# Banded attention in a fused transformer layer: the row maxima are transposed a unit later, behind the score products, and their products are moved a unit later

## The chip, the cores and the metric

The kernel runs on one core of one Trainium2 chip. The metric is the device time of one execution in microseconds. A profile of one execution shows each engine's instructions: PE (matmul), PEld (weight load), DVE, ACT, POOL and SP, which here only issues DMAs.

## What is computed

One layer of a transformer: modulation, RMSNorm, one input projection, two groups of attention heads, an output projection, a mixture of 16 experts, and a final norm. The change lies in head group A, banded attention with a sink in the softmax. For each block of 128 queries and each of 2 key groups (4 heads share the keys):

```python
keys = jnp.concatenate([kc, kb], axis=1)      # 256 context keys, 384 keys of the band
s = jnp.einsum('bqkgd,bskd->bkgqs', qb, keys) * (DH_A ** -0.5) + bias
p = jax.nn.softmax(jnp.concatenate([s, s_sink], axis=-1), axis=-1)[..., :-1]
o = jnp.einsum('bkgqs,bskd->bqkgd', p, vals)
```

Softmax needs a maximum of every query row before the exponential is taken.

## The kernel before

Banded attention is 16 blocks (8 of 128 queries for each key group; a block holds 4 heads, so 512 columns). A block is a run of 4 or 5 **units**, one for each 128 keys; there are 76 units. The numbers of a block's first unit are U0 = 0, 4, 9, 14, 19, 24, 29, 34, 38, 42, 47, 52, 57, 62, 67, 72.

`Runner.run` (L591) writes the instruction order by hand. In unit u it first emits what was registered for that unit (`at[u]`), then the unit's scores (`s_a`, L759), then the subtraction `lo` of the unit before, then the value products of unit u-3 (`pv_a`, L774). Every engine takes its instructions in the order in which they are emitted, and so does SP's queue of DMAs. An instruction that waits holds all that stands behind it on its engine.

The scores are two products, or three with the mask: L765 with the queries, L766 with a 65-row operand `ql` whose last row holds the negated maximum, and L768 with the mask. ACT then takes two exponentials (L614, L615). So **row 64 of `ql` has to be there before L766 of the block's first unit**.

`prep_blk(i)` (L665) makes that row, for block i while block i-2 is worked on, in nine steps. The list `OFFS` (L899) says at which unit after U0[i-2] each step stands; the three lists are for 10, 9 and 8 units from U0[i-2] to U0[i]:

- `tr`: 4 transposes on PE (L677), copy on ACT (L678). `low`: two DVE operations (L681, L682).
- `mxc(0)`, `mxb(0)`; `mxb(1)`; `mxc(1)`, `mxb(2)`; `mxb(3)`: six products on PE (L687, L695), each reduced to maxima on DVE (L689, L699).
- `fin`: two small DVE operations that give `nm` (L707, L708).
- `fin2`: PE transposes `nm` (L712), ACT copies it into `rr` (L714), SP issues two DMAs: `rr` into row 64 of `ql` (L715), and `rr` into `e` (L720).
- `fin3`: ACT takes the exponential of `e` (L724).

After the last value product of a block, `blk_finish` (L735) registers three steps. The product stands at unit U0+2 of the next block, and the steps 1, 3 and 6 units on: `s0` (a DMA from ACT's queue, L741), `s1` (DVE L744, L745; SP issues L746, then L748, which waits for L746 to land) and `s2` (POOL multiplies, L751; SP issues the block's output, L732, which waits for that). In terms of the block that is being prepared, `s2` of block i-3 stands at U0[i-2]+8.

All small PSUM tiles (`m`) share three banks in turn. The rest of the time goes to filling work in `at[u]`: in the first half the query up-projection `q_up` (L633) and `ka_prep` (L622), in the second `ckv_trans`, `kn_mm` and `v_mm`.

Of the kernel before, what the change touches and what calls it, by code (L numbers as in the profile page):

```python
# [38 lines left out]
def f32(ap):  # L39
    return ap.bitcast(F32)  # L40
# [7 lines left out]
def tile_backbone(ctx: ExitStack, tc, x, c, ctxt, c_ctx, w_mod, b_mod, norm_attn, norm_ffn, w_in,  # L48
# [107 lines left out]
    def bank(tag, shape=(128, 512)):  # L156
        return psa.tile(list(shape), F32, tag, bufs={"s": 3, "x": 2, "m": 3}[tag])
# [425 lines left out]
    class Runner:  # L583
# [4 lines left out]
        def add(self, u, f):  # L588
            self.at.setdefault(u, []).append(f)

        def run(self, units, emit_s, emit_pv, la):  # L591
            n = len(units)
            st = {}
            for u in range(n + la):
                self.u = u
                for f in self.at.pop(u, []):
                    f()
                if u < n:
                    st[u] = emit_s(u, units[u])
                if 1 <= u <= n:  # L600
                    st[u - 1][2]()
                if u >= la:
                    emit_pv(u - la, units[u - la], st.pop(u - la))
            late = [f for u in sorted(self.at) for f in self.at[u]]
            self.at = {}
            return late
# [48 lines left out]
    units = []  # L655
# [6 lines left out]
    HALF = U0[NT]  # L662
    R = Runner()

    def prep_blk(i):  # L665
        g, b = BL[i]
        st = {}

        def tr():
            st["q"] = q2 = pa.tile([128, 512], F32R, "q2", bufs=3)  # L670
            st["l"] = pa.tile([65, 512], F32R, "ql", bufs=3)
            st["x"] = pa.tile([128, 4, 2], F32, "mx", bufs=3)
            QA[i] = (q2, st["l"])
            pt = st["p"] = bank("m")
            for j in range(4):
                h = 4 * g + j
                pe.transpose(pt[0:64, j * 128:(j + 1) * 128], qa[:, b, h * 64:(h + 1) * 64], ident)  # L677
            act.activation(q2[0:64], pt[0:64], AF.Copy)  # L678

        def low():  # L680
            dve.tensor_copy(st["q"][64:128], f32(st["q"][0:64]))  # L681
            dve.tensor_sub(st["l"][0:64], st.pop("p")[0:64], f32(st["q"][0:64]))  # L682

        def mxc(a):
            pm = bank("m").rearrange("p (a b) -> p a b", a=2)
            for j in range(2):
                pe.matmul(pm[:, j], st["q"][:, (2 * a + j) * 128:(2 * a + j + 1) * 128], kst[g][:, 0:256],  # L687
                          start=True, stop=True)
            dve.tensor_reduce(out=st["x"][:, 2 * a:2 * a + 2, 0], in_=pm, axis=AX.X, op=OP.max)  # L689

        def mxb(j):
            j0, j1 = max(b - 1, 0), min(b + 2, NT)
            n = (j1 - j0) * 128
            pm = bank("m")
            pe.matmul(pm[:, :n], st["q"][:, j * 128:(j + 1) * 128],  # L695
                      kst[g][:, (NCT + j0) * 128:(NCT + j1) * 128], start=True, stop=True)
            junk = pa.tile([128, 384], F32, "mjunk")
            mo = j0 - (b - 1)
            dve.tensor_tensor_reduce(out=junk[:, :n], in0=pm[:, :n],  # L699
                                     in1=mq[:, mo:mo + (j1 - j0)].rearrange("p a b -> p (a b)"),  # L700
                                     scale=1.0, scalar=-3e38, op0=OP.add, op1=OP.max,
                                     accum_out=st["x"][:, j, 1:2])

        def fin():
            v = pa.tile([128, 4], F32, "mv", bufs=2)
            st["n"] = nm = pa.tile([128, 4], F32R, "nm", bufs=3)
            dve.tensor_max(v, st["x"][:, :, 0], st["x"][:, :, 1])  # L707
            dve.scalar_tensor_tensor(nm, v, -1.0, nsink8[:, 4 * g:4 * g + 4], op0=OP.mult, op1=OP.min)  # L708

        def fin2():  # L710
            pt = bank("m")
            pe.transpose(pt[:4, :128], f32(st["n"]), ident)  # L712
            rr = pa.tile([4, 128], F32R, "rr", bufs=2)
            act.activation(rr, pt[:4, :128], AF.Copy)  # L714
            nc.sync.dma_start(out=f32(st["l"][64:65, :]), in_=f32(rr))  # L715
            if i == len(BL) - 1:
                NM[i] = st["n"]
            else:
                E4[i] = pa.tile([128, 4], F32, "e4", bufs=3)
                nc.sync.dma_start(out=E4[i], in_=f32(rr))  # L720

        def fin3():
            if i < len(BL) - 1:
                act.activation(E4[i], E4[i], AF.Exp, scale=SC_A, bias=sinkp[:, g:g + 1])  # L724

        return [tr, low, lambda: (mxc(0), mxb(0)), lambda: mxb(1), lambda: (mxc(1), mxb(2)), lambda: mxb(3),
                fin, fin2, fin3]

    def blk_out(i, ou):
# [133 lines left out]
    def kr_pe(t0, t1):  # L863
        pt = bank("s")
        for t in range(t0, t1):
            pe.transpose(pt[:32, (t - t0) * 128:(t - t0 + 1) * 128], kr[:, t], ident)
        return pt
# [11 lines left out]
    def v_mm(t):  # L879
        pt = bank("m")  # L880
        for k in range(2):
# [5 lines left out]
    Q = [lambda t=t, g=g: q_up(t, g) for t in range(NT) for g in range(2)]  # L887
    CQ1 = [lambda k=k: cq_split(1, k, cq_pe(1, k, "m")) for k in range(3)]
    p0, p1 = prep_blk(0), prep_blk(1)
    NQP = 6  # L890
    pre = [Q[0], lambda: ka_prep(0, 0, 4), p0[0], Q[1], lambda: va_prep(0, 5), p0[1], p0[2], p0[3], Q[2], p0[4], p0[5],
           p1[0], Q[3], p0[6], lambda: ka_prep(0, 4, 8), p1[1], p0[7], Q[4],
           lambda: dve.tensor_copy(vah[:, :, :, 64], ones[:, 0:2 * NK].rearrange("p (a b) -> p a b", b=2)),
           p1[2], p1[3], last_scaled, p1[4], Q[5], p0[8]]
    for f in pre:
        f()
    for d, f in zip((0, 1, 1, 4), p1[5:]):
        R.add(d, f)
    OFFS = {10: (0, 1, 2, 3, 4, 5, 6, 7, 10), 9: (0, 1, 2, 3, 4, 5, 5, 6, 9), 8: (0, 1, 2, 2, 3, 4, 4, 5, 8)}  # L899
    for i in range(2, len(BL)):  # L900
        for d, f in zip(OFFS[U0[i] - U0[i - 2]], prep_blk(i)):
            R.add(U0[i - 2] + d, f)
# [12 lines left out]
        R.add(HALF + 3 + i * (len(units) - HALF - 5) // NKV, KV[i])  # L915
    KV = KV[NKV:]

    late = R.run(units, s_a, pv_a, 3)
    krt = [kr_pe(*g) for g in TG]
    for f in late:  # L920
        f()
# [96 lines left out]
    units = [(h, hf, kc, kc == 0, kc == NK - 1) for h in range(HB) for hf in range(2) for kc in range(NK)]  # L1018
# [803 lines left out]
```

## Time and profile before

| | |
|---|---|
| Time, median of 3 runs | 1213.65 us (1212.35 to 1213.77) |
| The profiled execution's own time | 1211.27 us |
| Its span, first to last instruction | 1209.6 us |
| PE busy | 1108.7 us (92% of the span) |
| DVE, ACT, POOL busy | 880.3, 702.6, 464.2 us |
| Banded attention, first to last score product | 232.5 to 401.5 us |

Busy time is a share of the whole span, over stages with different limits. For the change only the stage from 232 to 403 us matters, and the idle time of the engine that sets its pace.

### The profile page before, as it was taken

The numbers are of one execution on the slowest core, as the hardware profiler recorded it, in microseconds if no ns is written. First come the engines' busy times: TensorE is split into PE (matmuls) and PEld (weight loads), VectorE is DVE, ScalarE is ACT, GpSimd is POOL, SyncE is SP. The second block draws the span as 40 slices with busy tenths as digits, with TensorE's granted clock in tenths as the row PEclk, the third lists the DMA queues.
The fourth block names the chain that finished last, engine by engine and source line by source line (L and its number), as shares of the span: only waits on it lengthen the run. The fifth ranks groups of instructions, "written<-read, shape, count | busy, mean of one in ns | idle before, by whom it ended". The sixth has DMA issues, their size and how long they took to land. (4 is left out here: it accounts for less than half of the span.)

```text
span 1209.6 us, 15354 instructions
## 1 busy us (share of the span) xinstructions
PE 1108.7 (92%) x5168; PEld 833.1 (69%) x5168; DVE 880.3 (73%) x1509; ACT 702.6 (58%) x1124; POOL 464.2 (38%) x453
## 2 busy tenths in 40 slices
PE   7799998899899889999999999996499999999993
PEld 1587886677567667776766677885377887778871
DVE  5767764565884376776778255488789999999987
ACT  5633223467776567776776762323176776777754
POOL 0042221456443244665655432442214243332214
PEclk9899999899999999999999999997599999999997
DMA  8714320001211120212010535645799999999827
GB/s 303 286 67 132 116 90 1 1 15 23 62 28 23 27 85 22 88 53 88 19 44 16 182 91 200 236 187 218 277 324 368 376 363 390 373 394 370 290 44 286
DMA packets 68622, 198.27 MB, mean 164 GB/s; under 512 B 15894, under 2 KB 24243, under 8 KB 63423
## 3 DMA queue, kind: packets, MB, share of 16 engines
q1 hardware_dynamic: 60224, 178.73, 40.6%
q0 software_dynamic: 5152, 18.52, 5.8%
q8 instruction: 40, 0.66, 0.2%
q10 hardware_dynamic: 3168, 0.06, 0.1%
q14 instruction: 38, 0.31, 0.1%
HBM read 172.34 MB, written 24.78 MB: 163 GB/s over the span
## 5 line engine op out<-in xcount | busy, mean ns | idle before, releaser
L1417 DVE TENSOR_TENSOR wl<-wst,wh 128x2048 fp32r<-128x2048 f32 x95 | 216.1, 2289 | 22.2 <-ACT wh L1411 22.2
L1411 ACT ACTIVATE wh<-wst 128x2048 fp32r<-128x2048 f32 x96 | 183.9, 1917 | 71.7 <-PE u L1588 40.0
L614 ACT ACTIVATE ph<-s 128x512 fp32r<-128x512 f32 x236 | 140.7, 596 | 91.4 <-PE s L1103 74.1
L1106 POOL TENSOR_TENSOR pl<-pf,ph 128x512 fp32r<-128x512 f32 x76 | 102.3, 1356 | 64.9 <-ACT pf L615 53.2
L1106 DVE TENSOR_TENSOR pl<-s,ph 128x512 fp32r<-128x512 f32 x84 | 57.0, 680 | 54.1 <-ACT s L615 54.1
L986 DVE TENSOR_REDUCE mx<-m 128x1 f32<-128x512 f32 x128 | 83.1, 682 | 10.5 <-PE m L984 10.2
L615 ACT ACTIVATE s<-s 128x512 f32<-128x512 f32 x123 | 73.1, 594 | 0.0
L1634 PE MATMUL y<-wh,shf 128*128 128x512 f32 x240 | 69.4, 400 | 0.0
L1099 PE MATMUL s<-ql,kh 96*128 96x512 f32 x160 | 65.1, 407 | 2.7 <-DVE pl L1106 2.7
L772 POOL TENSOR_TENSOR pl<-pf,ph 128x512 fp32r<-128x512 f32 x37 | 47.5, 1285 | 50.6 <-ACT pf L615 47.3
L615 ACT ACTIVATE pf<-s 128x512 f32<-128x512 f32 x113 | 66.9, 592 | 0.0
L122 POOL TENSOR_SCALAR rstd<-ss 128x1 f32<-128x1 f32 x36 | 13.1, 363 | 134.9 <-ACT sjunk L193 65.2
L1103 PE MATMUL s<-qh,kh 97*128 97x512 f32 x160 | 63.3, 396 | 1.3 <-DMA qh<-rr 1.3
L1115 PE MATMUL x<-ph,vh 128*65 128x512 f32 x160 | 63.2, 395 | 0.0
L1100 PE MATMUL s<-qh,kl 96*128 96x512 f32 x160 | 63.1, 394 | 0.0
L1117 PE MATMUL x<-pl,vh 128*65 128x512 f32 x160 | 63.0, 393 | 0.0
L1116 PE MATMUL x<-ph,vh 128*64 128x512 f32 x160 | 62.9, 393 | 0.0
L329 PE MATMUL s<-wih,hb 128*128 128x512 f32 (+2 forms) x224 | 57.0, 376 | 3.2 <-ACT hb L81 3.2
L1556 POOL DMA_INDIRECT xg<-h2d,ix x16 | 23.6, 1472 | 91.5 <-PE t L1572 36.4
L1651 POOL DMA_INDIRECT accd<-yt,ix x7 | 34.7, 4958 | 61.2 <-DVE yt L1644 61.2
L81 ACT ACTIVATE hb<-xt 128x512 fp32r<-128x512 f32 (+1 forms) x22 | 13.0, 593 | 69.3 <-DVE xt L245 69.2
L984 PE MATMUL m<-kh,qh 96*128 96x512 f32 x128 | 47.0, 412 | 5.8 <-ACT kn L877 3.8
(491 smaller groups left out, 3105.7 us busy)
## 6 DMA issues: line engine op xcount, KB each, us to landing
wst<-in_w_gate_dram SPq DMA_DIRECT2D x63, 512.0 KB
wst<-in_w_up_dram SPq DMA_DIRECT2D x63, 512.0 KB
wst<-in_w_down_dram SPq DMA_DIRECT2D x31, 1024.0 KB
mw<-in_w_mod_dram SPq DMA_DIRECT2D x32, 256.0 KB
wst<-in_w_mod_dram SPq DMA_DIRECT2D x8, 1024.0 KB
wi<-in_w_in_dram SPq DMA_DIRECT2D x8, 720.0 KB
wi<-in_w_mod_dram SPq DMA_DIRECT2D x9, 512.0 KB
h2d<-h SPq DMA_DIRECT2D x8, 520.0 KB
```

What stands on the lines that cost most here:

```text
L614: act.activation(ph, ps, AF.Exp, scale=scale)
L615: act.activation(pf, ps, AF.Exp, scale=scale)
L986: dve.tensor_reduce(out=st["m"][:, t, j:j + 1], in_=pm, axis=AX.X, op=OP.max)
L1099: pe.matmul(ps, kh[0:96, ks], ql[:, qs], start=True, stop=False)
L1100: pe.matmul(ps, kl[:, ks], qh[0:96, qs], start=False, stop=False)
L1103: pe.matmul(ps, kh[:, ks], qh[:, qs], start=False, stop=True)
L1106: return ph, lo, lambda: (dve if on_dve else pool).tensor_sub(lo, pf, f32(ph))
L1115: pe.matmul(xx, vv[:, kc, 0:65], ph, start=first, stop=False)
L1117: pe.matmul(xx, vv[:, kc, 0:65], lo, start=False, stop=last)
L1411: act.activation(W[i][0], staged[i], AF.Copy)
L1417: eng.tensor_sub(lo, staged.pop(i), f32(hi))
L1634: pe.matmul(py[n], a[:, k], w[b][:, n], start=(k == 0 and m == 0), stop=(k == 3 and m == 2))
```

## The change

The step `fin2` no longer emits its instructions. It puts them (as `fin2b`) on a list, which `Runner.run` empties right behind the unit's scores. In the list of first steps ahead of the runner, the list is emptied after each step, so there the order is as before. The offsets in `OFFS` change: the products of the maxima stand up to a unit later, `fin` stands in the unit of the last of them, and `fin2` a unit later than before.

```diff
-        def run(self, units, emit_s, emit_pv, la):
+        def run(self, units, emit_s, emit_pv, la, between=None):
...
                 if u < n:
                     st[u] = emit_s(u, units[u])
+                if between:
+                    between()
                 if 1 <= u <= n:
                     st[u - 1][2]()
...
+    LATER = []
...
         def fin2():
+            LATER.append(fin2b)
+
+        def fin2b():
             pt = bank("m")
             pe.transpose(pt[:4, :128], f32(st["n"]), ident)
...
+    def after_s():
+        while LATER:
+            LATER.pop(0)()
+
     for f in pre:
         f()
+        after_s()
...
-    OFFS = {10: (0, 1, 2, 3, 4, 5, 6, 7, 10), 9: (0, 1, 2, 3, 4, 5, 5, 6, 9), 8: (0, 1, 2, 2, 3, 4, 4, 5, 8)}
+    OFFS = {10: (0, 1, 3, 4, 5, 6, 6, 8, 10), 9: (0, 1, 3, 4, 4, 5, 5, 7, 9), 8: (0, 1, 3, 3, 4, 4, 4, 6, 8)}
...
-    late = R.run(units, s_a, pv_a, 3)
+    late = R.run(units, s_a, pv_a, 3, after_s)
```

The third offset is that of the first products, the seventh that of `fin`, the eighth that of `fin2`, the ninth that of `fin3`.

## Rows read from the trace of the kernel before

**Rows 1.** Busy time by stage: the start and end of the stretch, its length, then for each engine the busy time and the number of instructions, the granted clock of PE, the DMA share and GB/s. The two halves of banded attention, and the dense attention after it.

```profile
232.00:318.00 86.00, 80.93 (x414) 58.71 (x413) 58.64 (x149) 63.01 (x131) 47.80 (x69) 1.00 0.10 18
318.00:403.00 85.00, 80.30 (x381) 55.79 (x380) 55.88 (x137) 62.10 (x126) 34.96 (x28) 0.98 0.17 39
435.00:730.00 295.00, 286.45 (x1282) 200.97 (x1281) 197.22 (x294) 208.51 (x384) 163.27 (x125) 1.00 0.23 75
```

**Rows 2.** What PE waited for from 215 to 402 us: us in total, times, longest.

```profile
PE m L712 <- DVE nm L708: 3.9, 5, 1.4
PE m L687 <- DVE q L681: 1.8, 5, 0.7
...
PE m L687 <- DVE ql L682: 1.0, 1, 1.0
PE m L637 <- ACT rr L714: 0.8, 2, 0.6
```

**Rows 3.** The same waits one by one, on PE's timeline (start, duration, engine, line, operation, tiles, shape, and in brackets the idle time before it and what ended it): a value product of block 0, and block 2.

```profile
237.94 0.44 PE L783 MATMUL x<-pl,vah 128*65 128x512 f32 x1 [0.70 <-POOL pl L772]
...
243.49 0.27 PE L712 MATMUL m<-ident,nm 128*4 128x128 f32 x1 [0.70 <-DVE nm L708]
```

**Rows 4.** PE's timeline, block 10's maxima.

```profile
331.30 0.27 PE L712 MATMUL m<-ident,nm 128*4 128x128 f32 x1 [1.44 <-DVE nm L708]
```

**Rows 5.** PE's timeline, block 12's time: a product of maxima that waits.

```profile
353.42 0.50 PE L687 MATMUL m<-ks,q 128*128 128x256 f32 x2 [0.66 <-DVE q L681]
```

**Rows 6.** All engines' timeline, block 11's maxima and the DMAs at the end of block 8.

```profile
341.18 0.32 SPq L746 DMA_DIRECT2D rcd<-l  x1
...
341.46 0.27 PE L712 MATMUL m<-ident,nm 128*4 128x128 f32 x1 [0.72 <-DVE nm L708]
...
342.64 0.49 SPq L748 DMA_DIRECT2D rbc<-rcd  x1
...
342.71 0.47 PE L687 MATMUL m<-ks,q 128*128 128x256 f32 x2 [0.98 <-DVE ql L682]
```

**Rows 7.** All engines' timeline: block 10's DMA behind another, unit 45's last exponential, and the product that needs the DMA.

```profile
334.73 0.46 SPq L748 DMA_DIRECT2D rbc<-rcd  x1
335.28 0.64 SPq L715 DMA_DIRECT2D ql<-rr  x1
...
335.61 0.59 ACT L615 ACTIVATE s<-s 128x512 f32<-128x512 f32 x1
...
337.81 0.40 PE L766 MATMUL s<-ql,k 65*128 65x512 f32 x1
```

**Rows 8.** PE's timeline, scores of unit 17 and of unit 19, the first of block 4.

```profile
273.05 0.40 PE L765 MATMUL s<-q,kn 128*128 128x512 f32 x1
...
278.43 0.40 PE L766 MATMUL s<-ql,vb 65*128 65x512 f32 x1
```

**Rows 9.** SP's timeline, the DMAs of block 4's maxima (L715, L720) and what follows them: L732 is the output of block 1.

```profile
268.44 0.64 SPq L715 DMA_DIRECT2D ql<-rr  x1
269.13 0.60 SPq L720 DMA_DIRECT2D e<-rr  x1
276.64 0.65 SPq L732 DMA_DIRECT2D mixd<-ou  x1
```

**Rows 10.** POOL's timeline, the product ahead of that output.

```profile
275.33 1.29 POOL L751 TENSOR_TENSOR ou<-ou,rbc 64x512 f32<-64x512 f32 x1
```

**Rows 11.** ACT's timeline: last exponential of unit 27, and `fin3` of block 6.

```profile
301.13 0.59 ACT L615 ACTIVATE s<-s 128x512 f32<-128x512 f32 x1
...
302.60 0.31 ACT L724 ACTIVATE e<-e,sinkp 128x4 f32<-128x4 f32 x1
```

**Rows 12.** PE's timeline: the first L766 of blocks 6 and 7.

```profile
301.72 0.40 PE L766 MATMUL s<-ql,vb 65*128 65x512 f32 x1
...
311.15 0.39 PE L766 MATMUL s<-ql,vb 65*128 65x512 f32 x1
```

**Rows 13.** SP's timeline: the DMAs at the end of block 4.

```profile
304.52 0.32 SPq L746 DMA_DIRECT2D rcd<-l  x1
306.48 0.49 SPq L748 DMA_DIRECT2D rbc<-rcd  x1
...
310.73 0.65 SPq L732 DMA_DIRECT2D mixd<-ou  x1
```

**Rows 14.** All engines' timeline, the output of block 8 and the first L766 of block 11.

```profile
347.67 0.65 SPq L732 DMA_DIRECT2D mixd<-ou  x1
...
350.15 0.39 PE L766 MATMUL s<-ql,k 65*128 65x512 f32 x1
```

**Rows 15.** All engines' timeline, block 14: last exponential of unit 65, and the first L766 of the block.

```profile
382.69 0.59 ACT L615 ACTIVATE s<-s 128x512 f32<-128x512 f32 x1
...
385.93 0.39 PE L766 MATMUL s<-ql,k 65*128 65x512 f32 x1
```

**Rows 16.** ACT's timeline there: `fin3` of block 4 and the copy that stands behind it.

```profile
276.55 0.30 ACT L724 ACTIVATE e<-e,sinkp 128x4 f32<-128x4 f32 x1
276.82 0.59 ACT L678 ACTIVATE q<-m 64x512 fp32r<-64x512 f32 x1
```

**Rows 17.** Busy time by stretch, columns as in Rows 1: before and in a stretch at half the clock.

```profile
338.00:343.70 5.70, 4.00 (x21) 2.43 (x20) 4.17 (x11) 3.96 (x9) 3.60 (x3) 1.00 0.12 23
343.70:347.10 3.40, 3.40 (x11) 2.09 (x10) 2.49 (x8) 2.15 (x4) 0.73 (x1) 0.50 0.15 47
```

## Prediction

> **What bounds the kernel now.** I read the stages first. Banded attention takes 171 us, and in both halves PE is the busiest engine, 80.93 of 86 and 80.30 of 85 us, while ACT, next, has 63.01 and 62.10. The dense attention behind it is bound by PE too, 286.45 of 295 us [rows 1]. So a microsecond that PE gains or loses in the banded stage should reach the end. I take it one to one; less is possible, more isn't shown.
>
> Then I read what PE waits for in this stage. 3.9 us go to the transposition of the maxima, which stands on PE ahead of DVE's result. 1.8 and 1.0 us go to the first products of the maxima, which wait for the lower halves of the queries, and 0.8 us to a PSUM bank that the copy `rr` held: 7.5 us in all [rows 2]. That is the most that the change can take away. Last I read, block by block, what stands behind those waits: SP's queue, ACT's queue and the time at which the maxima are needed.
>
> **What the change removes.** The transposition gets a unit more behind `fin`, and the products a unit more behind `low`, so these waits [rows 2] should go. No operation is added or dropped. But a wait that is gone is only time won if nothing else ends at the same moment:
> - Block 1's wait is followed by a value product that waits 0.70 us for POOL [rows 3]. POOL doesn't hang on PE there, so that wait grows by what is saved: 0.
> - Block 2: 0.70 us [rows 3], kept.
> - Block 10: 1.44 us [rows 4], kept. Block 12: 0.66 us [rows 5], kept.
> - The rest of the 1.8 us at L687 is some 1.1 us. About 0.3 lies in blocks 6 and 7, treated below; I keep 0.8.
> - Block 11: 0.72 and 0.98 us [rows 6]; see below.
> - The 0.8 us at the bank of `rr` I leave out. The copy comes later, and other holders of the banks come later too (the copy of `tr` below). The bounds are a gain of 0.8 and a loss of 1.5 us (0.5 in three blocks).
>
> Kept: 0.70 + 1.44 + 0.66 + 0.8 = 3.6 us.
>
> **What it moves, and past what.** `fin2` isn't one instruction but four: transposition, copy on ACT, two DMAs on SP. Each is queued behind more than before. On PE it stands behind the scores of unit U0-2, on ACT behind that unit's two exponentials, and on SP behind whatever that unit has issued. For blocks with 10 units this includes the output L732 of block i-3, which stands in the same unit, ahead of the scores, and waits for POOL. In the kernel before the maxima's DMAs were ahead of it. The new wait is L766 of the block's first unit, for row 64 of `ql`, and behind it on PE stand the value products.
>
> How long does such a DMA take to land? No row gives it for `ql` itself. L746 is a DMA of the same 2 KB, and L748 waits for it: 341.18 to 342.64, 1.46 us [rows 6]. That is the lower bound. Block 10's `ql` was issued at 335.28 and used at 337.81 without a wait, so 2.53 is the upper bound [rows 7]. I take 1.75: the nearer row, plus 0.3 for an issue that takes 0.64 us on SP where the other takes 0.32.
>
> The Trainium skill (DMA: Bandwidth & Descriptors, on the anatomy of one DMA) gives about 2.0 us as the fixed cost of a DMA on another issuing path, most of it the receipt of the write. By that the sum below would be some 1.5 us higher, an estimate from six late landings of 0.25 us more. The row of L746 shows a shorter one, 1.46 us, and the sum goes by the rows.
>
> Blocks 3, 4 and 5, where `q_up` fills the units: take block 4. Unit 17's scores start at 273.05 and the first L766 of the block at 278.43 [rows 8]. Before, the DMA was issued at 268.44; the output L732 is issued at 276.64 [rows 9], when POOL's product, 275.33 and 1.29 us long, is done [rows 10]. Now the DMA follows it at 276.64 + 0.69 = 277.33 and lands at 279.08. PE waits 279.08 - 278.43 = 0.65 us. Blocks 3 and 5 have the same order of steps and filling work: **3 x 0.65 = 1.95 us**.
>
> Blocks 6 and 7, where `ka_prep` keeps ACT busy: unit 27's last exponential ends at 301.13 + 0.59 = 301.72 [rows 11], so `rr` is ready at 301.97, and the DMA lands at 302.0 + 1.75 = 303.75. L766 stood at 301.72 [rows 12]: 2.0 us. ACT loses too: `fin3` stood at 302.60 and waits for `e`, whose DMA is issued 0.7 us behind the other: 302.7 + 1.75 = 304.45, so 1.85 us [rows 11]. Behind it on ACT stand the copies that DVE waits for ahead of `s1` of block 4. The chain from L746 at 304.52 to the output at 310.73 [rows 13] is DMAs and POOL; 1.85 us later the output ends at 310.73 + 1.85 + 0.65 = 313.2 less some 0.5 us that L748 had waited behind other work, so 312.7, and block 7's DMA lands at 314.5. L766 stood at 311.15 [rows 12]. So by block 7 PE is **3.4 us** late, block 6's 2.0 included, and the waits that were there before (some 1.1 us) are swallowed. Bounds: +1.5 (ACT catches up) and +5.
>
> Block 10: unit 45's last exponential ends at 336.20, so `rr` is ready at 336.45 and lands near 338.2, against 337.81 [rows 7]: **0.4 us**. Block 11: the output of block 8 hangs on a chain from 341.18 [rows 6] and leaves at 347.67; the DMA behind it lands at 348.36 + 1.75 = 350.1, just when L766 stood, 350.15 [rows 14]. So the 1.70 us saved ahead of it turn into a wait for the DMA: net **0**.
>
> Blocks 12 to 15 have cover. The thinnest is block 14: the last exponential ends at 383.28, `rr` at 383.53, landing at 385.3, use at 385.93 [rows 15]. What hides it is 0.6 us of other products; without that cover it costs up to 1.1 us by the upper bound of the landing. `fin3` waits about 1 us for `e` on ACT in these blocks, which has idle time there: 0, with up to 0.4 us a block if it isn't enough.
>
> **The sum.** +1.95 + 3.4 + 0.4 - 3.6 = +2.15 us. The profiled execution took 1211.27 us (span 1209.6), so it would take 1213.4 by itself. That execution is 2.4 us below the median of the runs, 1213.65, so I add to the median: **1215.8 us**. A measurement of this kernel can tell about 0.2%, 2.4 us, from no change; +2.15 lies within. The stage gains at one place and loses at another. By the ends of the landing (1.46 and 2.53 us, six late ones) the sum is +0.4 or +6.8.
>
> **The rivals.**
>
> *Slower: ACT stands at `fin3`, and PE's new waits bring its clock down.* `e` lands 2.7 us and more behind the moved issue. In block 4 that is 277.33 + 0.7 + 1.75 = 279.8 against 276.55, so ACT stands 3.2 us [rows 16]. Behind it stand the copy of `tr` for block 6 [rows 16], which holds one of the three banks, the copy of `q_up`, and the exponentials. Where DVE's `low` comes so late that the third taker of the banks waits, PE loses about 0.5 us a block. In the six blocks 3 to 7 and 10, where the landing is late, that is 3 us more. It decides from the point where ACT's wait at `fin3` is longer than the two units PE has before the bank is taken again. And after the stretch in which PE was busy for 4.00 of 5.70 us, the granted clock is 0.50, 1.2 instead of 2.4 GHz, for 3.40 us, in which PE issues 11 products [rows 17]; half of that stretch, 1.7 us, is lost. The waits at blocks 6 and 7 could cause one more. That is +2.15 + 3 = +5.15, with the clock +6.85: 1218.8 to 1220.5; I give 1219. For it speaks that ACT's order is strict; against it that ACT has 23 us idle in each half [rows 1].
>
> The Trainium skill (TensorE: Matmul & The Clock Gate, Part 1) says that an idle PE drops to its lower level. The row at 343.7 us agrees; no row here tells whether the new, shorter waits are enough.
>
> *Faster: the DMAs land in time.* If PE comes to the uses later than I think, or POOL's product earlier, the late landings cost half, 5.75 / 2 = 2.9 us, and the waits saved at block 11 and at the bank (1.7 + 0.8) are kept as well. That is 2.9 - 3.6 - 2.5 = -3.2, and -4.9 if the fall of the clock at 343.7 us goes with the waits ahead of it [rows 17]: 1208.7 to 1210.5; I give 1209.5. For it: 7.5 us of waits are seen, the new ones are only worked out. Against it: SP's order, which the rows show at work. Block 10's DMA went out right behind L748 [rows 7].
>
> *The change doesn't do what it says*: PE's waits only move to the next instruction that needs DVE (as in block 1), and no landing is late: 1213.65. It is part of the middle case.
>
> **How the numbers follow.** Within 0.2% by my sum or by the last rival: 0.41. Slower, by the first rival or by the upper ends of landing and blocks 6 and 7: 0.37. Faster, by the second: 0.22. The likeliest is my sum, 1215.8. Both signs hold much of the chance, so the range reaches to both rivals, 1209 to 1220.5; the sum's own range, by the ends of the landing, is 1214 to 1220.5.
>
> **What would show it.** In the profile of the changed kernel: no wait for `nm` at L712 and nearly none for L681 at L687. New idle time on PE ahead of L766, ended by a DMA of `ql`, 0.5 to 1 us in blocks 3, 4 and 5, 2 us in block 6, 2 to 3 in block 7 and some 2 in block 11. On SP the DMAs of `ql` come right behind L732 in blocks 3, 4, 5, 7 and 11. On ACT idle time of 1 to 3 us ahead of L724, ended by a DMA of `e`. The prediction is wrong if L766 never waits (then SP's order isn't what I read), or if the waits at L712 are still there, or if the time between the scores of units 17 and 19 has changed.

## The result, and the profile after

The changed kernel takes 1226.41 us (median of 4 runs, 1224.49 to 1228.77) against 1213.71 us for the kernel before in the same comparison: a ratio of 1.0108 [1.0088, 1.0129], 12.7 us slower. The time lies outside the predicted range (1209.0 to 1220.5). The profiled executions, one of each kernel, differ by 14.8 us (1226.07 against 1211.27). Of these, 0.9 us lie ahead of banded attention, 11.1 in it and 2.9 behind it. I measure **the stage** from the first score product to the start of the last L773 (L766 before): 169.06 us before, 180.14 after. In this stage, line numbers of the changed kernel are 2 to 7 higher.

Lines of the page of the changed kernel: the span, and the busy time of each engine.

```profile
span 1224.4 us, 15348 instructions
PE 1120.6 (92%) x5168; PEld 838.6 (68%) x5168; DVE 880.7 (72%) x1509; ACT 702.0 (57%) x1124; POOL 465.4 (38%) x453
```

Its stages, columns as in [rows 1]: the two halves, and a stretch at half the clock.

```profile
232.00:318.00 86.00, 77.68 (x388) 55.63 (x386) 53.60 (x139) 57.70 (x121) 45.90 (x67) 0.99 0.09 17
318.00:414.00 96.00, 89.86 (x403) 60.78 (x404) 60.47 (x146) 65.96 (x136) 36.17 (x29) 0.95 0.16 36
...
342.40:349.20 6.80, 6.11 (x19) 3.84 (x18) 5.68 (x12) 2.96 (x7) 1.44 (x2) 0.50 0.08 21
```

In the same 86 us PE gets through 388 products instead of 414, and 77.68 us are busy instead of 80.93 (some of that is the stage's start, 0.9 us later). The operations are the same; what is new must be waiting, or a lower clock. What PE waits for from 215 to 425 us:

```profile
PE s L773 <- DMA ql<-rr: 3.9, 3, 2.2
PE s L772 <- ACT pf L617: 1.3, 2, 1.0
PE m L691 <- DVE q L685: 1.2, 2, 0.7
PE m L681 <- ACT rr L721: 1.0, 1, 1.0
PE m L628 <- DVE ks L631: 1.0, 1, 1.0
PE x L790 <- POOL pl L779: 1.0, 2, 0.8
PE m L719 <- DVE mx L693: 0.7, 1, 0.7
```

Beside [rows 2] the change did what it says: the 3.9 us for `nm` are gone, and of 2.8 us at the first products 1.2 are left. In their place stand the DMA of `ql` and waits of takers of the three banks for operations on ACT and DVE that read the last holder (`rr`, `ks`, `mx`); PE's idle time in the stage rises from 9.77 to 14.46 us. The larger new wait is not PE's. Two rows of what ACT waits for:

```profile
ACT e L731 <- DMA e<-rr: 29.0, 12, 4.2
ACT qb L642 <- PE m L639: 9.3, 6, 4.4
```

**ACT stands 29.0 us ahead of `fin3`, in 12 blocks.** Before it was 0.6 us, and none of it for `e`. Some of that comes out of ACT's idle time: its wait for `qb` was 15.0 us before and is 9.3 now. In block 4 this goes as follows. SP's timeline, where the output L739 now leads:

```profile
277.14 0.66 SPq L739 DMA_DIRECT2D mixd<-ou  x1
277.90 0.64 SPq L722 DMA_DIRECT2D ql<-rr  x1
278.59 0.59 SPq L727 DMA_DIRECT2D e<-rr  x1
```

ACT's timeline, block 4, then block 9:

```profile
275.46 0.25 ACT L721 ACTIVATE rr<-m 4x128 fp32r<-4x128 f32 x1
...
276.45 0.59 ACT L617 ACTIVATE pf<-s 128x512 f32<-128x512 f32 x1
280.86 0.30 ACT L731 ACTIVATE e<-e,sinkp 128x4 f32<-128x4 f32 x1 [3.82 <-DMA e<-rr]
281.06 0.58 ACT L682 ACTIVATE q<-m 64x512 fp32r<-64x512 f32 x1
...
337.65 0.30 ACT L731 ACTIVATE e<-e,sinkp 128x4 f32<-128x4 f32 x1 [3.14 <-DMA e<-rr]
337.85 0.58 ACT L682 ACTIVATE q<-m 64x512 fp32r<-64x512 f32 x1
338.33 0.67 ACT L861 ACTIVATE cvh<-m,vc 128x512 fp32r<-128x512 f32 x1
338.90 0.58 ACT L616 ACTIVATE ph<-s 128x512 fp32r<-128x512 f32 x1
339.38 0.59 ACT L617 ACTIVATE pf<-s 128x512 f32<-128x512 f32 x1
```

PE's timeline, the first L773 of blocks 3, 4 and 7, then what follows block 9's `fin3`:

```profile
266.23 0.50 PE L773 MATMUL s<-ql,vb 65*128 65x512 f32 x1 [0.20 <-DMA ql<-rr]
...
277.58 0.44 PE L639 MATMUL m<-wqh,vb 128*128 128x384 f32 x1 [0.17 <-DVE mx L693]
...
279.25 0.40 PE L772 MATMUL s<-q,kn 128*128 128x512 f32 x1
279.72 0.50 PE L773 MATMUL s<-ql,vb 65*128 65x512 f32 x1
...
318.40 0.70 PE L773 MATMUL s<-ql,vb 65*128 65x512 f32 x1 [2.18 <-DMA ql<-rr]
...
340.02 0.51 PE L772 MATMUL s<-q,ks 128*128 128x512 f32 x1 [0.98 <-ACT pf L617]
...
342.13 0.53 PE L691 MATMUL m<-ks,q 128*128 128x256 f32 x2 [0.66 <-DVE q L685]
...
345.86 0.38 PE L719 MATMUL m<-ident,nm 128*4 128x128 f32 x1 [0.69 <-DVE mx L693]
```

Two chains can be read here. On SP the output was issued at 276.64 before, *behind* block 4's two DMAs at 268.44 and 269.13 [rows 9]; now they follow it, 9.5 us later, though `rr` is there from 275.71 (275.46 + 0.25). On ACT `fin3` kept its place (276.55 before [rows 16]), so ACT stands 3.82 us until 280.86. In block 9 what stands behind it is plain: the copies at 337.85 and 338.33 and the exponentials at 338.90 and 339.38 all start late, PE's L772 waits 0.98 us for the last, its L691 0.66 us for DVE, and from 342.4 to 349.2 us the granted clock is 0.50.

The Trainium skill (TensorE: Matmul & The Clock Gate, Part 1) says that a PE left idle drops to the lower of its two levels, 1.2 GHz; the fall behind those waits agrees with it. But idle time in sum doesn't decide it: in experiment 8 below PE is idle for 15.69 us of the stage, longer than here, and the clock doesn't fall there. What sets a fall off, no run here shows.

### The profile page after: what moved, and what is told of

Its sections match the earlier page's. It is cut to its first block, busy times and chain, and to the rows that moved or that the text cites. A ratio compares the mean times of both kernels' runs of the same rounds, so it can differ in the third digit from the quotient of the medians.

```text
span 1224.4 us, 15348 instructions
## 1 busy us (share of the span) xinstructions
PE 1120.6 (92%) x5168; PEld 838.6 (68%) x5168; DVE 880.7 (72%) x1509; ACT 702.0 (57%) x1124; POOL 465.4 (38%) x453
## 5 line engine op out<-in xcount | busy, mean ns | idle before, releaser
L998 DVE TENSOR_REDUCE mx<-m 128x1 f32<-128x512 f32 x128 | 83.1, 683 | 10.6 <-PE m L996 10.2
L703 DVE CUSTOM_DVE_ANT_0 mjunk<-m,mq 128x384 f32<-128x384 f32 (+1 forms) x64 | 33.1, 517 | 28.3 <-PE m L699 27.0
```

The costliest lines, as they stand in the source:

```text
L998: dve.tensor_reduce(out=st["m"][:, t, j:j + 1], in_=pm, axis=AX.X, op=OP.max)
```

## The experiments

**The theories.** A: ACT stands at `fin3` until `e` lands, and what is queued behind (copies, exponentials) frees banks late; PE loses there. B: on SP the DMA of `ql` is queued behind the output, L773 waits for its landing, and ACT plays no part. "Stage" is that of the profiled execution, one each; kernels whose medians can't be told from the one before have stages of 168.3 to 170.7 us, so 1.5 us more or less says little. In the comparisons below, single runs of the kernel before go from 1205.7 to 1219.5 us, and a ratio is known to 0.2 or 0.3%. The medians of the kernel before are 1212.04 us beside experiments 1 to 4, 1210.76 beside 5 to 8 and 1211.46 beside 9 to 11.

**1. `fin3` two units later** (else as changed):

```diff
-    OFFS = {10: (0, 1, 3, 4, 5, 6, 6, 8, 10), 9: (0, 1, 3, 4, 4, 5, 5, 7, 9), 8: (0, 1, 3, 3, 4, 4, 4, 6, 8)}
+    OFFS = {10: (0, 1, 3, 4, 5, 6, 6, 8, 12), 9: (0, 1, 3, 4, 4, 5, 5, 7, 11), 8: (0, 1, 3, 3, 4, 4, 4, 6, 10)}
```

> The changed kernel with fin3 (ACT's exponential of e) two units later, so that ACT reaches it after e has landed; nothing else moves. Theory A (most of the loss comes from ACT standing at fin3, which makes the copies, exponentials and banks behind it late): 6 us or more of the 12.7 come back, 1216 to 1220 us. Theory B (the loss comes from PE standing at L766 for the late row of ql, and from the clock that falls with it): at most 2 us come back, 1224 to 1227 us, and the waits at L766 are as before.

**2. The output a unit later** (else as changed), so that on SP it follows the DMAs of `ql` and `e`:

```diff
             pool.tensor_mul(ou[0:64], ou[0:64], st["r"])
+
+        def s3():
             blk_out(i, ou)
-        return list(zip((1, 3, 6), (s0, s1, s2)))
+        return list(zip((1, 3, 6, 7), (s0, s1, s2, s3)))
```

> The changed kernel with the output DMA L732 of blk_finish one unit after POOL's product instead of in the same unit, so that on SP the DMAs of ql and e are ahead of it. Theory B: the waits at L766 shrink to those of block 6, 5 us or more come back, 1217 to 1221 us. Theory A: e comes earlier too by some 2 us in blocks 3, 4, 5, 7 and 11, half of ACT's wait at fin3 stays, 3 to 6 us come back, 1220 to 1223 us. If neither hangs on SP's order: 1225 to 1227 us.

**3. Both edits together.**

> Both: fin3 two units later and L732 a unit later. If A and B are the whole cause together, what is left is the late rr in block 6 (2 us) against the 3.6 us of waits saved: 1210 to 1215 us. If something third costs time (the place of the products of the maxima, the banks): 1217 us or more.

Measured: 1 takes 1215.73 us, a ratio of 1.0028 [1.0006, 1.0050], stage 172.71 us; 2 takes 1217.50, 1.0036 [1.0015, 1.0058], stage 175.32; 3 takes 1213.91, 1.0020 [0.9994, 1.0046], stage 169.47. One row each: what PE waits for in 1, what ACT waits for in 2, what PE waits for in 3:

```profile
PE s L773 <- DMA ql<-rr: 1.9, 2, 1.5
```

```profile
ACT e L731 <- DMA e<-rr: 20.1, 12, 3.2
```

```profile
PE s L775 <- DMA ql<-rr: 1.3, 1, 1.3
```

In 1 and 3 ACT doesn't stand at `fin3` at all. So both theories hold, each for a part. Of the stage's 11.1 us, A's edit takes back 7.4, B's 4.8, and both 10.7. The medians show the same, but not the same shares: of the 1.08%, 1 takes back 0.80, 2 0.72 and both 0.88, each known to some 0.3. The edits overlap, by more than the stage's 1.5 us if the medians are right: an output that leaves later also lets `e` land earlier (29.0 to 20.1 us of standing in 2). Neither theory alone explains all of it, and which of them costs more is not shown.

How the stage's time splits into PE's idle time and its clock can be read from rows, columns as in [rows 1]. In this order: the stage of the kernel before, of the changed kernel, and of 1, 2, 5, 8 and 9. PE's idle time is the length less PE's busy time.

```profile
232.47:401.53 169.06, 159.29 (x783) 113.20 (x781) 113.68 (x283) 123.86 (x256) 81.69 (x95) 0.99 0.14 29
233.35:413.49 180.14, 165.68 (x783) 114.97 (x781) 113.70 (x283) 122.51 (x255) 81.81 (x95) 0.97 0.13 27
231.50:404.21 172.71, 162.16 (x784) 114.00 (x781) 115.67 (x283) 123.82 (x256) 82.11 (x96) 0.99 0.13 28
231.18:406.50 175.32, 161.64 (x784) 113.03 (x781) 117.19 (x283) 123.10 (x256) 81.37 (x95) 1.00 0.12 28
230.91:407.50 176.59, 163.23 (x784) 115.14 (x782) 111.37 (x283) 122.38 (x256) 81.30 (x95) 0.97 0.12 28
231.41:405.70 174.29, 158.60 (x784) 111.81 (x781) 120.06 (x283) 125.34 (x256) 81.27 (x95) 1.00 0.14 28
231.15:401.07 169.92, 158.45 (x783) 112.19 (x781) 114.30 (x283) 124.25 (x256) 81.99 (x95) 1.00 0.14 29
```

At half the clock are 3.4 us of the stage before, 10.2 of the changed kernel's, 3.4 of 1's and none of 2's; half of such time is lost where PE sets the pace. So 1 takes back 3.9 us of PE's idle time (14.46 to 10.55) and 3.4 of clock, while 2 takes back 0.8 of idle time (to 13.68) and 5.1 of clock. The clock also differs between executions of one kernel: in the 31 runs before beside 1 to 4, its mean over the whole run goes from 0.956 to 0.970. So the shares of a single stage hold some luck, B's 4.8 us most of all.

**4. The transposition back in its old unit**, still behind the scores, products as changed:

```diff
-    OFFS = {10: (0, 1, 3, 4, 5, 6, 6, 8, 10), 9: (0, 1, 3, 4, 4, 5, 5, 7, 9), 8: (0, 1, 3, 3, 4, 4, 4, 6, 8)}
+    OFFS = {10: (0, 1, 3, 4, 5, 6, 6, 7, 10), 9: (0, 1, 3, 4, 4, 5, 5, 6, 9), 8: (0, 1, 3, 3, 4, 4, 4, 5, 8)}
```

> The changed kernel with fin2 in its old unit (7, 6, 5 units after U0[i-2]), still behind the scores of that unit; products of the maxima and fin as changed. The DMAs are ahead of L732 on SP and a unit earlier on ACT. Theories A and B both: the landing is in time in most blocks, the saved waits of 2 to 4 us stay, 1209 to 1214 us. If the new place of the products is what costs: 1218 us or more.

Measured: 1218.55 us, 1.0052 [1.0029, 1.0074], stage 177.68 us. ACT stands only 7.2 us at `fin3`, yet the expected gain isn't there. PE waits again, for `nm` and at the bank of the products:

```profile
PE m L719 <- DVE nm L712: 4.1, 3, 2.3
PE s L773 <- DMA ql<-rr: 1.9, 2, 1.5
PE m L699 <- DVE mx L693: 1.9, 2, 1.0
```

That was a miss for both theories; the time is that of the third case, in which the new place of the products costs. Experiments 7 and 8 take that up.

**5 and 6. One late DMA alone, in the kernel before.** In 5 only the DMA of `e` is issued a unit later, behind the scores (blocks 2 to 14; the last block has no `e`); in 6 only that of `ql`, in the same manner (blocks 2 to 15). 5's edit (6 wraps the DMA into `ql` in the same way):

```diff
...
-                nc.sync.dma_start(out=E4[i], in_=f32(rr))
+                e_in = lambda: nc.sync.dma_start(out=E4[i], in_=f32(rr))
+                if i < 2:
+                    e_in()
+                else:
+                    LATER.append((R.u + 1, e_in))
...
+    def after_s(u):
+        for f in [f for v, f in LATER if v <= u]:
+            f()
+        LATER[:] = [(v, f) for v, f in LATER if v > u]
...
```

> The kernel before with one thing changed: the DMA of rr into e (L720) is issued a unit later, behind the scores of that unit (so behind L732 on SP); ql's DMA stays. It measures theory A alone. Theory A: ACT waits at fin3 as in the changed kernel (2 to 4 us in blocks 3, 4, 5, 7, 9, 11) and the time rises by 5 to 9 us, to 1219 to 1223. Theory B: ACT's wait is covered, rise under 2 us.

> The kernel before with one thing changed: the DMA of rr into ql (L715) is issued a unit later, behind the scores (so behind L732 on SP); e's DMA stays early. It measures theory B alone, without the part that comes from a later rr. Theory B: PE waits at L766 in blocks 3, 4, 5, 7 and 11, rise of 5 to 9 us, 1219 to 1223. Theory A: rise of 1 to 3 us, 1214.5 to 1217.

Measured: 5 takes 1218.12 us, 1.0056 [1.0031, 1.0081], stage 176.58 us, 7.5 more than before; 6 takes 1217.69, 1.0048 [1.0027, 1.0069], stage 174.60, 5.5 more. What ACT waits for in 5, one row of what PE waits for there, and what PE waits for in 6:

```profile
ACT e L732 <- DMA e<-rr: 16.5, 6, 3.4
```

```profile
PE m L639 <- ACT rr L718: 1.9, 3, 0.9
```

```profile
PE s L774 <- DMA ql<-rr: 7.0, 6, 2.2
```

In 5 no L774 (the old L766) waits for a DMA, and ACT's standing alone makes the kernel slower: the copies behind it come late, and PE waits 1.9 us at a bank that `rr` held (0.8 before [rows 2]). Of the 7.5 us, 3.6 are PE's idle time and 3.4 its clock (10.2 us at half). In 6 ACT stands 0.3 us, and PE's new wait alone makes the kernel slower, with no more time at half the clock than before (3.4 us). Each mechanism is shown without the other, at about the size that 1 and 2 gave (7.4 and 4.8).

**7. Only the place behind the scores**: the changed kernel with the `OFFS` of the kernel before.

```diff
-    OFFS = {10: (0, 1, 3, 4, 5, 6, 6, 8, 10), 9: (0, 1, 3, 4, 4, 5, 5, 7, 9), 8: (0, 1, 3, 3, 4, 4, 4, 6, 8)}
+    OFFS = {10: (0, 1, 2, 3, 4, 5, 6, 7, 10), 9: (0, 1, 2, 3, 4, 5, 5, 6, 9), 8: (0, 1, 2, 2, 3, 4, 4, 5, 8)}
```

> The kernel before with fin2 behind the scores of its old unit, all steps at their old offsets: the first half of the change without the second. PE no longer stands at L712 ahead of the scores, rr comes behind one unit's exponentials. By both theories the DMAs are still in time (a unit earlier than in the changed kernel, ahead of L732): 1209 to 1213 us, the gain being the 3.9 us at L712 less block 1 and block 11.

**8. Only the later products**: `OFFS` as in 4, and the transposition at once instead of behind the scores.

```diff
         def fin2():
-            LATER.append(fin2b)
+            fin2b()
...
```

> The kernel before with the products of the maxima and fin at their new offsets, fin2 at its old unit and ahead of the scores: the second half of the change alone. The waits at L687 (2.8 us) go, those at L712 may grow since fin is no earlier. By A and B: 1211 to 1215 us. If the place of the products is the cause of the loss: 1218 us or more.

Measured: 7 takes 1212.36 us, 1.0017 [0.9997, 1.0037], stage 170.67 us; 8 takes 1218.61, 1.0046 [1.0017, 1.0074], stage 174.29. What PE waits for in 7 and in 8:

```profile
PE m L691 <- DVE q L685: 7.2, 7, 1.9
```

```profile
PE m L719 <- DVE nm L712: 9.5, 11, 1.7
```

7 lies in the range that I gave, but the gain isn't there. Its waits for `nm` are gone, but the wait at the next product that needs DVE, the first of the maxima, grows from 1.8 to 7.2 us. 8 came out as its second case, the place of the products: later products make `nm` later, and PE waits 9.5 us for it instead of 3.9, in 11 blocks. So the change's two parts need each other: the later products make the transposition wait, and a transposition late enough not to wait makes `ql` and `e` late.

**9. Control for 5**: 5, with `fin3` two units later.

```diff
-    OFFS = {10: (0, 1, 2, 3, 4, 5, 6, 7, 10), 9: (0, 1, 2, 3, 4, 5, 5, 6, 9), 8: (0, 1, 2, 2, 3, 4, 4, 5, 8)}
+    OFFS = {10: (0, 1, 2, 3, 4, 5, 6, 7, 12), 9: (0, 1, 2, 3, 4, 5, 5, 6, 11), 8: (0, 1, 2, 2, 3, 4, 4, 5, 10)}
```

> Control for the run with e's DMA late alone: the kernel before with e's DMA a unit later, behind L732, and fin3 two units later as well. If what cost time there was ACT standing at fin3 (theory A), the cost goes: 1209 to 1214 us, same as before. If it was the changed order on SP, or the late e itself: 1216 us or more.

Measured: 1213.84 us, 1.0017 [0.9994, 1.0039], stage 169.93 us. A row of L732 (`fin3`) in 9: all 15, and the view lists no idle time ahead of any.

```profile
L732 ACT ACTIVATE e<-e,sinkp x15: 280/297/303, 231.2 to 389.7; 128x4 f32<-128x4 f32 x15
```

The same late DMA costs 7.5 us of the stage where `fin3` stays, and 0.9, within what such stages differ by, where it is moved with it. So 5's cost comes with ACT's standing and not with the DMA's time. Of the 6.6 us between the two stages 5.1 are clock, which doesn't fall in 9's; the medians tell 5 and 9 apart too, but only just (0.4%, known to some 0.3).

**10 and 11. Two tries at a gain.** 10: transposition behind the scores in its old unit, `fin3` later, and only the first products later (where blocks are 8 units apart, the second product too). 11: products as before, transposition behind the scores in its old unit, `fin3` two units later, the output a unit later as in 2 (its `OFFS` is that of 9).

```diff
-    OFFS = {10: (0, 1, 3, 4, 5, 6, 6, 8, 10), 9: (0, 1, 3, 4, 4, 5, 5, 7, 9), 8: (0, 1, 3, 3, 4, 4, 4, 6, 8)}
+    OFFS = {10: (0, 1, 3, 3, 4, 5, 6, 7, 12), 9: (0, 1, 3, 3, 4, 5, 5, 6, 11), 8: (0, 1, 3, 3, 3, 4, 4, 5, 10)}
```

> A version that should keep the gain and pay neither cost: fin2 behind the scores of its old unit (ahead of L732 on SP), fin3 two units later, fin at its old unit, and of the products of the maxima only the first pair a unit later, so that it is behind low. If the gain is there to be had: the waits at L712 and L687 go and 2 to 5 us are won, 1207 to 1210 us. If the products now crowd the three banks: the waits move to the instructions that take a bank, 1211 to 1214 us.

> fin2 behind the scores of its old unit, fin3 two units later, L732 a unit later, all products at their old offsets. No DMA is late and ACT doesn't stand at fin3; the waits at L687 for the lower half of the queries stay or grow, since PE no longer waits at L712 before them. 1209 to 1213 us: the saving at L712 mostly turns into the wait at L687.

Measured: 10 takes 1212.49 us, 1.0005 [0.9987, 1.0023], stage 170.53 us; 11 takes 1212.91, 1.0001 [0.9983, 1.0020], stage 168.31. What PE waits for in 10 and in 11:

```profile
PE m L860 <- DVE mx L693: 2.5, 3, 1.1
PE m L699 <- DVE mx L693: 1.6, 2, 0.9
```

```profile
PE m L691 <- DVE q L685: 6.4, 8, 1.1
```

Neither beats the kernel before. ACT waits for `e` nowhere, and for `nm` PE waits 0.2 and 0.5 us. The waits have moved: in 10 to takers of a bank whose reductions on DVE aren't done, in 11 to the first products. The lists of waits say so; that DVE's order is what would have to change was not tried.

## Why the prediction was wrong

**Failed: `fin3` put at 0.** The prediction worked out that ACT would stand 3.2 us at `fin3` in block 4 (measured 3.82), but the sum charged such a wait in blocks 6 and 7 only. Elsewhere it counted on ACT's 23 us of idle time, and left the wait to a rival, "ACT stands at `fin3`", at 3 us. The mechanism of that rival is what happened, and its price is the term that was mis-sized: 7.4 us by experiment 1, 7.5 by experiment 5. About half of it is idle time of PE, 3.9 and 3.6 us, near the 3 us of the rival; the other half is clock, 3.4 us each, twice the one fall of 1.7 us that the rival allowed. ACT's idle time was no cover, because it isn't one stretch that a wait can be put into: it lies between inputs, and in block 9 what stood behind `fin3` was already due. Whether the falls of the clock come with the standing in every execution, one profile of each kernel doesn't show.

**Also too small: the landing of `e`.** It was taken as 1.75 us like that of `ql`. From L727's issue to `fin3` it is 2.16 to 2.84 us in the 12 blocks (block 4: 278.59 to 280.86, 2.27). For `ql` 1.75 was near: 1.82 in block 4 (277.90 to 279.72) and in block 7 (316.58, by SP's timeline, to 318.40).

**Right: SP's order.** L722 follows L739 at once, 277.14 to 277.90, where I had 276.64 and 277.33. The Trainium skill (DMA: Bandwidth & Descriptors, on the anatomy of one DMA) says that a wait for a semaphore is taken by the sequencer that issues the DMA, ahead of it. These rows agree: L739 waits for POOL, and `ql`, which doesn't need POOL and whose `rr` is there from 275.71, leaves 0.76 us behind it.

**Term by term**, from how much later than before each block's first L773 starts, counted from the first score product:

| Blocks | predicted us | measured us |
|---|---|---|
| 2 (wait kept) | -0.70 | -0.6 |
| 3, 4, 5 | +1.95 | +1.5 |
| 6, 7 | +3.4 (bounds 1.5 and 5) | +5.2 |
| 8, 9 | 0 | +1.8 |
| 10 | +0.4 - 1.44 | +3.7 |
| 11 | 0 | -1.4 |
| 12 to 15 | -0.66 | +0.6 |

The other 0.8 us predicted at L687 have no block. In blocks 3 to 5 the sum came out near, but in part by luck. L773 was to wait 0.65 us in each; idle time ahead of it is listed for block 3 alone, 0.20 us, and in block 4 it starts 0.47 us behind L772, where 0.23 is usual (314.11 and 314.34 us). PE comes to it later than predicted: unit 17's first product starts at 273.55, so from there to L773 it is 6.17 us, 5.38 before [rows 8]. That this time changed is one of the prediction's own signs of being wrong. Part of what PE lost on the way is a wait at a bank (L639, 0.17 us in block 4).

Blocks 6 and 7 came out at the upper bound, where late `e` and late `ql` meet. In block 7 L773 waits 2.18 us, as predicted, but in block 6 the 2.0 us are not there: no idle time is listed ahead of its L773, and PE stands at the banks instead (1.0, 1.0 and 0.5 us, for `ks`, `rr` and `mx`). Block 8 has a stretch at half the clock (318.5 to 321.9 us) right behind the wait in block 7. Block 10 missed by 4.8 us: its stretch holds block 9's `fin3`, the waits behind it (0.98, 0.66 and 0.69 us) and the 6.8 us at half the clock, of which half is lost. Block 11's -1.4 us holds the 1.7 that the kernel before lost there to its own fall [rows 17]; without it the forecast of 0 is near.

In all, half the clock lasts 10.2 us in the stage, 3.4 before [rows 17]: 3.4 us lost. PE's longer idle time is another 4.7. The other 3.0 of the 11.1 us I can't name by rows one by one. A stop costs more than the idle time listed for it, as L773 in block 4 shows, and PE stops more often; whether that makes up the 3.0 was not worked out.

**The waits that should turn into a gain** did go, but the sum kept 3.6 us of them as won time. Experiments 7 and 11 remove the waits for `nm` nearly without late landings (in 7 PE waits 1.0 us at L773 and ACT 2.5 at `fin3`, in 11 neither is listed) and gain nothing that can be measured. So that step, too, was too hopeful; the rival "waits only move to the next instruction that needs DVE" describes 7. For the later products the prediction had no price at all; experiment 8 gives 5.2 us of the stage when they stand alone.

The other signs: no wait for `nm` (right); idle time ahead of L773 ended by the DMA (right in blocks 7 and 11, 2.18 and 1.52 us; 0.20 in block 3, and none listed in 4, 5 and 6); ACT idle ahead of `fin3` (right, up to 4.2 us where I had 1 to 3).

## What to carry to other kernels

Whoever moves a step must move everything that waits for its results: here `fin2` went a unit later and `fin3` stayed, and that alone cost about as much as all the waits that were to be won (7.5 us; by the medians of 5 some 7). Idle time of an engine with a strict order hides a wait only if nothing due stands behind the waiting instruction; list those instructions and who waits for each before a wait is put at zero. A wait taken off a bound engine is won only if the next instruction that needs the same producer isn't due as well: with DVE late, PE's wait for `nm` became one for `q` or for a bank.

## What was not expected of the hardware

Two DMAs of the same 2 KB from the same source, issued 0.7 us apart on SP's queue, take unlike times from issue to use: into one row of `ql` 1.82 us (blocks 4 and 7), into 4 elements in each of 128 rows of `e` 2.27 and 2.36 us there and 2.16 to 2.84 us in the 12 blocks. Why was not tested.
